# The sample's pointwise product: sixteen plain jobs of one token half each, or four units of seven block products

## The chip, the core and the metric

The kernel runs on one core of a Trainium2 chip. The metric is the device time of one execution in microseconds; three runs of the kernel before gave 2074.37, 2077.41 and 2079.27 us, and their median, 2077.41 us, is the time before.

## What is computed

One encoder layer is applied to two sequences that share all weights: a "sample" of 1024 tokens and a "prompt" of 512. All in fp32.

```python
def conformer_conv(u_val, u_glu, w_dw, b_dw, ln_g, ln_b, w_pw):
    h = u_val * jax.nn.sigmoid(u_glu)
    h = depthwise_conv(h, w_dw, 31 taps) + b_dw          # 1024 channels
    h = jax.nn.silu(layer_norm(h, ln_g, ln_b))
    return h @ w_pw                                       # 1024 x 1024

def mixer_layer(x, ...):
    z = rms_norm(x, norm_g) @ w_in                        # 2048 -> 5632
    c_val, c_glu, c_gate, q, k, v, a_gate = split(z)
    conv_out = conformer_conv(c_val, c_glu, ...) * silu(c_gate)
    attn_out = banded_sink_attention(rope(q), rope(k), v, sink) * silu(a_gate)
    return x + concat([conv_out, attn_out]) @ w_out       # 2048 -> 2048

y = rms_norm(mixer_layer(x), final_norm_g)                # for sample and prompt
```

The change is about `h @ w_pw`, the pointwise product, of the sample alone.

## The kernel before

**Layout and precision.** Channels lie on the 128 partitions, tokens along the free dimension. Every fp32 operand of a product is split into a high and a low part (`Encoder.parts`, L506: ScalarE copies the rounded high part at L510, VectorE subtracts it at L511), and a product of two blocks is three matmuls: high by high, high by low, low by high. Weights come as raw tiles of 512 KB (`raw`, 3 buffers) and become split tiles (`hl`, 3 buffers); split tokens are `t` tiles of 128 x 2 x 512 (`T1`, L456, 28 buffers). Other buffers: `f` (7 of 4 KB a partition), `a` (4), `g` and `u` (4 each of 2 KB a partition); `E()` (L477) hands out `g` and `u` in turn.

**Two ways to multiply.** A `Job` (L386) is one output block of 128 columns for 512 tokens: `Encoder.run` (L641) issues 3 matmuls for each input block, at L670. A `Unit` (L94) makes two column blocks for both halves of the sample's tokens from 8 input blocks, seen as a 2 x 2 by 2 x 2 block product, with seven products instead of eight (Winograd's form). Its token sums are S1 = A21 + A22, S2 = S1 - A11, S3 = A11 - A21, S4 = A12 - S2 (A12: first token half, second half of the input blocks). Its weight sums are made by VectorE from the two raw tiles (`sub`, L142-L163). Each of the seven products, in the order P1, P2, P6, P5, P7, P3, P4, is 4 input blocks x 3 matmuls of 512 columns, at L207. Three PSUM banks accumulate them, and after each product a `tap` (L230) takes the bank out: ScalarE copies (L236) and VectorE adds (L257); P7's bank is read before P4 accumulates into it one product later. `Onto` (L271) is the unit of the output projection: its four results start from tiles that GpSimd's queue loads, and VectorE adds every bank into them (L304).

**Order of the work.** The sample's input projection comes first (units, to about 850 us), then the prompt's 44 jobs `pj`, then the sample's pointwise product, then the sample's output projection (`over[0]`, `over[1]`: 16 `Onto` units), then the prompt's pointwise product and its output projection. Everything beside the products is written as generators in three lanes (`Lane`, L64). After every three matmuls `tick` (L517) gives each lane 648 ns times its rate of credit, and a lane steps while it has credit; each `yield` costs what it names. The lane `prep` runs at rate 1, `conv` (the prompt's depthwise taps, L1004) at 0.5 here, `attn` first sums up the sample's attention output (`attention_sums`, L1291: four rounds that each fill all four `a` tiles), then runs the prompt's attention (L1152). What weights and taps need is emitted with high priority; lane instructions stand behind it on VectorE and ScalarE. Every plain load and store goes over SP's queue in a fixed order; each engine's queue is in order too.

**The pointwise product of the sample.** From `pj[18]` (`prepare`, L2052) the `prep` lane runs `Post.prepare` (L1448) for each token half: layer norm and silu of the convolution's output, ending in a store to `cs_d` (L1500). Then `fetch` (L1505) loads the first half's 8 blocks back and splits them. For each half come 8 jobs (`first_jobs`, L1547): job i loads weights `w_pw[i]` (L404), the gate (`load_gate`, L1539), and multiplies the bank by the gate on VectorE (`pointwise`, L1530-L1533), then stores into `mix_d`. While the first half's jobs run, the second half is fetched; while the second half's run, `Mix.fill` (L1333) splits four of the seven token lots (4 tiles each) that the output projection's first unit needs; `rest` and the hooks after it (L2082-L2089) make the other three.

Of the kernel before, what the change touches and what calls it, by code (L numbers as in the profile page):

```python
# [7 lines left out]
F32 = mybir.dt.float32  # L8
F32R = mybir.dt.float32r
AF = mybir.ActivationFunctionType  # L10
ALU = mybir.AluOpType
PSUM = bass.MemoryType.PSUM

P = 128
# [26 lines left out]
LEAD = 9000  # L41
SPREAD = 3
RATES = (0.4, 0.6, 0.3, 1.0, 0.5)
S1, S2, S3, S4, S5, S6, S7, S8 = 5000, 6000, 9000, 7000, 3500, 2500, 6000, 6000
# [226 lines left out]
class Onto(Unit):  # L271
# [29 lines left out]
    def tap(self, name):  # L301
        n = self.START.get(name) or self.REST[name]
        d = self.d[n]
        self.e.nc.vector.tensor_tensor(d, self.bank[BANK[name]], d, ALU.add)  # L304
        if name in self.REST or name == "P4":
            del self.d[n]
            if self.total:
                self.done(n[0], n[1], d)
            else:
                self.e.store(self.part[n[0]][n[1]], d)  # L310


# [951 lines left out]
class Mix:  # L1264
# [67 lines left out]

    def fill(self):  # L1333

        e = self.e
        e.T = {}
        held = deque()

        def load(step):
            if step < 7:  # L1340
                held.append(self.load_sum(SUMS[ALONE[step]], 1, True, e.F))

        def put(step):
            for j, x in enumerate(held.popleft()):
                self.token_sum(SUMS[ALONE[step]], 1, j, x)

        load(0)
        load(1)
        for step in range(4):
            yield 2 * LOAD  # L1350
            put(step)
            load(step + 2)
        self.put, self.load = put, load

    def units(self):
        e = self.e
        out = []
        for o in range(0, ND, 2):
# [13 lines left out]
            out.append(one)  # L1372
        return out

    def project(self, o, t, z):
# [60 lines left out]


class Post:

# [3 lines left out]
    def __init__(self, e, seq, t0, out):  # L1443
        self.e, self.seq, self.t0, self.out = e, seq, t0, out
        self.cs, self.mix, self.made = {}, {}, {}
        self.cs_d = [e.tc.dram_tile([P, 2, self.N], F32, name=f"cs{seq.s}_{t0}_{i}") for i in range(NC // 2)]

# [51 lines left out]
    def normed(self, i, t):  # L1499
        self.e.store(self.cs_d[i], t)  # L1500
        self.kept = i + 1

    kept = 0

    def fetch(self):  # L1505

        e = self.e
        held = deque()

        def load(i):  # L1510
            if i < NC // 2:
                held.append(e.F([2, self.N]))
                e.nc.sync.dma_start(held[-1], self.cs_d[i])

        load(0)
        load(1)
        for i in range(NC // 2):
            yield LOAD
            t = held.popleft()
            load(i + 2)  # L1520
            for j in (0, 1):
                self.cs[2 * i + j] = self.parts(t[:, j])
                yield 1500

    def parts(self, f):
        t = self.e.T1([2, self.N])
        self.e.parts(t[:, 0], t[:, 1], f)
        return t

    def pointwise(self, i, acc):  # L1530
        e, nc = self.e, self.e.nc
        f = self.gates.pop(i)
        nc.vector.tensor_tensor(f, acc[0], f, ALU.mult)  # L1533
        self.mixed(i, f)

    def mixed(self, i, f):
        self.e.store(self.out.xT[i][:, self.t0 : self.t0 + self.N], f)

    def load_gate(self, i):  # L1539
        e = self.e  # L1540
        if i == 0:
            self.gates = {}
        f = e.G()
        e.nc.sync.dma_start(f, self.seq.gate_d[i][:, self.t0 : self.t0 + self.N])
        self.gates[i] = f

# [328 lines left out]
def encoder(ctx, tc, a):  # L1875
    e = Encoder(ctx, tc, a)
    sample, prompt = Sequence(e, 0), Sequence(e, 1)
    mix = Mix(e, sample, a["y_s"])
    halves = [Post(e, sample, 0, mix), Post(e, sample, TP, mix)]
    last = LastPost(e, prompt, 0, a["y_p"], mix.wsum_d)  # L1880
# [171 lines left out]
    def prepare():  # L2052
        until(lambda: sample.convolved == NC, e.conv)
        for half in halves:
            e.prep.add(half.prepare())
        e.prep.add(halves[0].fetch())
        e.attn.add(mix.attention_sums(prompt.fetch_first))
        for group in prompt.groups:
            e.attn.add(group)
# [6 lines left out]

    for n, half in enumerate(halves):
        fj = half.first_jobs()
        fj[0].before.insert(0, lambda half=half: until(lambda: len(half.cs) == NC, e.prep))
        if n == 0:  # L2070
            fj[0].before.append(lambda: e.prep.add(halves[1].fetch()))
        else:

            def fill():
                until(lambda: mix.gated == HALF, e.attn)
                e.prep.add(mix.fill())

            fj[0].before.append(fill)
        jobs += [[j] for j in fj]
    out = mix.units()  # L2080
    over = [[u(1, False) for u in out], [u(0, True) for u in out]]
    def rest():  # L2082
        e.prep.drain()
        mix.put(4)

    over[0][0].before.append(rest)
    over[0][0].after[0] = [lambda: (mix.put(5), mix.load(6))]
    over[0][0].after[1] = [lambda: e.prep.add(mix.conv_sums())]
    over[0][0].after[3] = [lambda: mix.put(6)]  # L2089
    over[0][-1].before += [e.prep.drain, e.attn.drain]  # L2090
# [17 lines left out]
    over[1][0].next = None  # L2108
    fj[-1].before.append(lambda: chain[0].begin((0, 0)))

# [67 lines left out]
```

## Time and profile before

| | |
|---|---|
| median of three runs | 2077.41 us |
| the profiled execution: its own time / its span | 2079.13 us / 2077.4 us |
| TensorE matmuls | 9256 recorded, busy 2060.1 us |
| VectorE / ScalarE / GpSimd busy | 1728.4 / 1081.8 / 157.9 us |
| DMA | 494.56 MB, mean 238 GB/s |
| sample's pointwise product on TensorE | from 1436.00 to 1536.06 us of the span |

The profile gives times in us from the start of the span. A matmul's end is modelled, so a run of matmuls is read by its starts. A row of the timeline is: start, duration, engine, line, operation, output <- inputs, how many were merged, and in brackets how long the engine sat idle before it and what ended that. A row of the stretches is: stretch, its length, busy time and count of each engine, granted clock, busy share of the 16 DMA engines, GB/s. A row of the groups is: line, engine, operation, shapes, count | busy us, mean ns of one | idle us before them and what ended it.

### The profile page before, as it was taken

To read this page: it belongs to the slowest core of one execution; us is meant where nothing else is said; L and a number is where in the kernel's file an instruction comes from. 1 tells how busy PE (TensorE), PEld (TensorE's weight loads), DVE (VectorE), ACT (ScalarE), POOL (GpSimd) and SP (SyncE) were. 2 spreads that over 40 slices of the span, in tenths; PEclk is the share of its full clock that TensorE was granted. 3 is DMA by queue.
4 is the path that set the end of the run, shared out by engine and by line. 5 is a ranking of instruction groups with operands and counts; after the bars stand their busy time and mean duration, and the time that the engine had idled before them with its cause. 6 is when DMAs were issued, how large, how long until landed. Compare 5 with 4: busy or idle time off the path is not lost.

```text
span 2077.4 us, 27223 instructions
## 1 busy us (share of the span) xinstructions
PE 2060.1 (99%) x9256; PEld 1697.9 (82%) x9256; DVE 1728.4 (83%) x2843; ACT 1081.8 (52%) x1771; POOL 157.9 (8%) x240
## 2 busy tenths in 40 slices
PE   9999999999999999999999999999999999999998
PEld 8888888888888888788888888888888887888886
DVE  8768899998899899889766777776799978998877
ACT  7486445333465555655555777336553343454454
POOL 0111111111112111100000000000000111100000
PEclk9999999999999999999999999999999999999999
DMA  8888886864577777954555555997789898778897
GB/s 285 309 300 256 200 215 226 286 218 158 190 243 197 181 167 179 279 167 158 164 183 185 178 172 188 316 329 233 239 295 295 279 324 283 213 259 277 293 324 279
DMA packets 242300, 494.56 MB, mean 238 GB/s; under 512 B 23664, under 2 KB 84464, under 8 KB 242160
## 3 DMA queue, kind: packets, MB, share of 16 engines
q1 hardware_dynamic: 216352, 428.83, 62.1%
q0 software_dynamic: 24512, 61.88, 12.5%
q10 hardware_dynamic: 1296, 2.11, 0.3%
q8 instruction: 72, 1.18, 0.2%
q14 instruction: 68, 0.56, 0.1%
HBM read 331.77 MB, written 160.96 MB: 237 GB/s over the span
## 4 chain that ended last, share of the span: by engine, by line
PE 73%; issue 8%; DMA 8%; DVE 7%; ACT 2%; POOL 1%; SPq 0%; ACTq 0%; POOLq 0%; DVEq 0%
PE a L207 21%; PE a L670 13%; PE c L207 10%; PE b L670 6%; PE c L670 6%; PE b L207 5%; PE s L1169 2%; PE pv L1198 2%; PE a L1852 2%; PE s L207 2%; DVE hl L511 2%; PE pt L1203 1%; PE s L1852 1%; DVE t L511 1%; DMA p<-y_d 1%
## 5 line engine op out<-in xcount | busy, mean ns | idle before, releaser
L207 PE MATMUL a<-t,hl 128*128 128x512 f32 x2640 | 632.5, 390 | 1.8 <-ACT u L236 1.3
L207 PEld LDWEIGHTS a<-t,hl 128*128 128x128 f32 x2640 | 493.5, 188 | 108.4 <-ACT u L236 2.4
L511 DVE TENSOR_TENSOR hl<-raw,hl 128x1024 fp32r<-128x1024 f32 (+3 forms) x334 | 337.8, 1012 | 151.5 <-ACT hl L510 147.3
L510 ACT ACTIVATE hl<-raw 128x1024 fp32r<-128x1024 f32 (+3 forms) x334 | 296.8, 889 | 314.4 <-PE c L207 88.1
L670 PE MATMUL a<-t,hl 128*128 128x512 f32 x1344 | 326.3, 393 | 0.0
L207 PE MATMUL c<-t,hl 128*128 128x512 f32 x1320 | 319.1, 389 | 0.0
L670 PEld LDWEIGHTS a<-t,hl 128*128 128x128 f32 x1344 | 248.8, 188 | 50.4
L207 PEld LDWEIGHTS c<-t,hl 128*128 128x128 f32 x1320 | 247.4, 188 | 51.5 <-DVE u L304 0.2
L1041 DVE SCALAR_TENSOR_TENSOR f<-f,c_w_dw,f 128x512 f32<-128x512 f32 x248 | 172.9, 744 | 0.2
L670 PE MATMUL b<-t,hl 128*128 128x512 f32 x672 | 162.9, 392 | 1.5 <-DVE t L515 0.8
L670 PE MATMUL c<-t,hl 128*128 128x512 f32 x672 | 163.9, 393 | 0.0
L1004 DVE SCALAR_TENSOR_TENSOR f<-f,c_w_dw,f 128x512 f32<-128x512 f32 x232 | 163.4, 742 | 0.2
L207 PE MATMUL b<-t,hl 128*128 128x512 f32 x660 | 159.8, 389 | 0.0
L670 PEld LDWEIGHTS b<-t,hl 128*128 128x128 f32 x672 | 124.8, 188 | 27.5 <-DVE t L515 1.1
L670 PEld LDWEIGHTS c<-t,hl 128*128 128x128 f32 x672 | 124.6, 188 | 24.8
L207 PEld LDWEIGHTS b<-t,hl 128*128 128x128 f32 x660 | 123.7, 188 | 25.6
L1033 DVE SCALAR_TENSOR_TENSOR f<-f,w_both,f 128x512 f32<-128x512 f32 x120 | 89.8, 748 | 2.0
L236 ACT ACTIVATE u<-a 128x512 f32<-128x512 f32 x82 | 48.8, 595 | 77.3 <-PE a L207 70.6
L236 ACT ACTIVATE g<-a 128x512 f32<-128x512 f32 x78 | 46.5, 596 | 78.5 <-PE a L207 68.5
L1183 ACT ACTIVATE p<-p,tiny 128x384 f32<-128x384 f32 (+1 forms) x96 | 54.6, 570 | 45.9 <-DVE tiny L1180 36.2
L510 ACT ACTIVATE a<-pt 128x512 fp32r<-128x512 f32 x64 | 38.0, 593 | 64.6 <-PE pt L1203 64.4
L285 POOL DMA_DIRECT2D g<-xT_s x16 | 8.8, 551 | 743.1 <-DMA att_d<-u 669.0
(356 smaller groups left out, 2765.2 us busy)
## 6 DMA issues: line engine op xcount, KB each, us to landing
raw<-w_in SPq DMA_DIRECT2D x170, 512.0 KB, 5.2
raw<-w_out SPq DMA_DIRECT2D x31, 512.0 KB, 5.1
raw<-w_pw SPq DMA_DIRECT2D x24, 512.0 KB, 4.2
wsum_P<-raw SPq DMA_DIRECT2D x47, 256.0 KB, 3.6
raw<-wsum_P SPq DMA_DIRECT2D x18, 512.0 KB, 5.1
f<-x_s SPq DMA_DIRECT2D x16, 512.0 KB, 8.5
g<-wsum_P SPq DMA_DIRECT2D x28, 256.0 KB, 4.6
a<-sum_S SPq DMA_DIRECT2D x24, 256.0 KB, 6.1
```

Of the source, the lines that this page charges most:

```text
L207: nc.tensor.matmul(acc, hl[:, l, o, j, :], toks[j][:, r], start=name in FRESH and j == 0 and q == 0, stop=name in LAST and j == HALF - 1 a ...
L236: nc.scalar.activation(t, bank, AF.Copy)
L510: nc.scalar.activation(hi, x, AF.Copy)
L511: nc.vector.tensor_tensor(lo, x, hi.bitcast(F32), ALU.subtract)
L670: nc.tensor.matmul(job.acc[0], hl[:, l, kk // HALF, kk % HALF, :], r, start=i == 0 and p == 0, stop=i == nk - 1 and p == 2,)
L1004: nc.vector.scalar_tensor_tensor(t, h[:, j : j + T], w(j), t, ALU.mult, ALU.add)
L1033: nc.vector.scalar_tensor_tensor(m0, odd[:, j : j + H], both(j), m0, ALU.mult, ALU.add)
L1041: nc.vector.scalar_tensor_tensor(out, d[:, j : j + H], w(2 * j + k), out if j else m0, ALU.mult, ALU.add)
L1169: nc.tensor.matmul(ps[:, 0:n], qs[:, x, h], k[y][:, keys], start=p == 0, stop=p == 2)
L1183: nc.scalar.activation(p[:, 0:n], p[:, 0:n], AF.Exp, bias=nm[:, h : h + 1], accum_out=l[:, h : h + 1])
L1198: nc.tensor.matmul(pv, v[x][:, vs], pt[:, y], start=i == 0 and p == 0, stop=i == last and p == 2)
L1852: nc.tensor.matmul(acc[t], self.toks[name, m][:, x, i, t * P : (t + 1) * P], parts[i][l].rearrange("p a b -> p (a b)"), start=fresh and fi ...
```

## The change

The sample's pointwise product is made by four units, one for each two columns of `w_pw`, over both token halves at once. A new class `Gated` (a `Unit`) loads the gates itself, two products ahead, over SP's queue, multiplies each finished result by its gate and stores it. A new class `Pointwise` holds the normed convolution's output in DRAM (`cs_d`), makes the sums S1 to S4 of block pairs by the generator that `Mix` has for its own (`conv_sums`, L1313: two loads of 512 KB, four VectorE operations, four stores of 256 KB for each of four pairs) and splits the first three token lots (`AHEAD`) while the prompt's jobs run; the last four lots are split before the first unit and after its first three products. The generators `fetch` and `fill` are gone; the output projection's token lots are split lot by lot behind the products of the last pointwise unit and the first output unit (`turn`). `conv_sums` of the output projection starts one product later.

```diff
+AHEAD = 3
+class Gated(Unit):
+    late = True
+    LASTS = {"P2": (0, 0), "P7": (1, 1), "P3": (0, 1), "P4": (1, 0)}
...
+    def begin(self, n):
+        self.g[n] = self.e.E()
+        self.e.nc.sync.dma_start(self.g[n], self.gate(*n))
+    def product(self, step, late):
+        if step == 0:
+            self.begin((0, 0))
+        name = self.order[min(step + 2, len(self.order) - 1)]
+        n = self.LASTS.get(name)
+        if n and n not in self.g:
+            self.begin(n)
+        return super().product(step, late)
+    def tap(self, name):
+        if name == "P4":
+            e, n = self.e, self.LASTS[name]
+            g = self.g[n]
+            e.nc.vector.tensor_tensor(g, self.bank[BANK[name]], g, ALU.mult)
+            e.store(self.to(*n), g)
+            self.g = {}
+        else:
+            super().tap(name)
+    def finish(self, n):
+        e, d = self.e, self.d.pop(n)
+        e.nc.vector.tensor_tensor(d, d, self.g[n], ALU.mult)
+        e.store(self.to(*n), d)
...
-    def fill(self):
...
+    def turn(self, unit, nxt, g):
+        held = {}
+        def load(step):
+            if step < 7:
+                held[step] = self.load_sum(SUMS[ALONE[step]], g, True, self.e.F)
+        def follow(step):
+            for j, x in enumerate(held.pop(step)):
+                self.token_sum(SUMS[ALONE[step]], g, j, x)
+            load(step + 2)
+        unit.before.append(lambda: (load(0), load(1)))
+        for step in range(7):
+            u, at = (unit, step + 2) if step < 5 else (nxt, step - 5)
+            u.after.setdefault(at, []).append(lambda step=step: follow(step))
...
+class Pointwise:
...
+    scale_of, sums_in_place, block_pairs = Mix.scale_of, Mix.sums_in_place, Mix.conv_sums
...
+    def ahead(self):
+        yield from self.block_pairs()
+        self.e.T = {}
+        self.load(0)
+        self.load(1)
+        for step in range(AHEAD):
+            yield 2 * LOAD
+            self.put(step)
+            if step + 2 < AHEAD:
+                self.load(step + 2)
+        self.ready = True
+    def units(self):
...
+        out = [one(i) for i in range(0, NC, 2)]
+        out[0].before.append(lambda: (self.put(AHEAD), self.load(AHEAD + 2)))
+        for step in range(AHEAD + 1, 7):
+            out[0].after[step - AHEAD - 1] = [lambda step=step: (self.put(step), self.load(step + 2))]
+        return out
...
     def normed(self, i, t):
-        self.e.store(self.cs_d[i], t)
+        for j in (0, 1):
+            self.e.store(self.out.xT[2 * i + j][:, self.t0 : self.t0 + self.N], t[:, j])
-    def fetch(self):
...
-        e.prep.add(halves[0].fetch())
+        e.prep.add(point.ahead())
...
+    def first_tokens():
+        until(lambda: point.ready, e.prep)
+        point.load(AHEAD)
+        point.load(AHEAD + 1)
+    pj[-2].before.append(first_tokens)
+    pw = point.units()
+    pw[-1].before.append(lambda: until(lambda: mix.gated == HALF, e.attn))
+    jobs += [[u] for u in pw]
...
+    mix.turn(pw[-1], over[0][0], 1)
+    over[0][0].after[2] = [lambda: e.prep.add(mix.conv_sums())]
...
+    pw[-1].after.setdefault(5, []).append(lambda: chain[0].begin((0, 0)))
```

## The prediction on record

> **What bounds the kernel.** I read the page first, its busy shares and its clock, then the stretches around the place of the change, then single matmuls in the timeline.
>
> ```profile
> span 2077.4 us, 27223 instructions
> PE 2060.1 (99%) x9256; PEld 1697.9 (82%) x9256; DVE 1728.4 (83%) x2843; ACT 1081.8 (52%) x1771; POOL 157.9 (8%) x240
> PEclk9999999999999999999999999999999999999999
> ```
>
> TensorE is busy in all but 17 us of the span, at full clock. VectorE, with 83%, is next. A busy TensorE may still be a slow one, so the second look is at its pace inside the stage that the change rewrites.
>
> ```profile
> 1525.18 5.60 PE L670 MATMUL c<-t,hl 128*128 128x512 f32 x24
> 1530.62 5.60 PE L670 MATMUL a<-t,hl 128*128 128x512 f32 x24
> 1536.06 2.88 PE L207 MATMUL a<-t,hl 128*128 128x512 f32 x12
> 1538.78 1.52 PE L207 MATMUL b<-t,hl 128*128 128x512 f32 x6
> ```
>
> The last two pointwise jobs start 5.44 us apart: 5.44/24 = 0.2267 us a matmul. The first product of a unit, 12 matmuls, takes 2.72 us to the next start: the same 0.2267. So neither form waits, and only fewer matmuls, or fewer waits elsewhere, can shorten the kernel. The stretches show what runs beside them.
>
> ```profile
> 1300.00:1350.00 50.00, 50.00 (x223) 41.39 (x222) 36.56 (x52) 15.96 (x19) 0.00 (x0) 1.00 0.91 314
> 1350.00:1400.00 50.00, 48.73 (x220) 40.08 (x219) 34.47 (x54) 16.28 (x22) 0.00 (x0) 1.00 0.94 333
> 1400.00:1436.00 36.00, 36.00 (x166) 30.10 (x165) 23.87 (x46) 25.14 (x44) 0.00 (x0) 1.00 0.70 228
> 1436.00:1536.00 100.00, 100.00 (x465) 83.31 (x464) 82.15 (x135) 53.34 (x93) 1.70 (x3) 1.00 0.79 264
> 1536.00:1600.00 64.00, 63.59 (x288) 51.04 (x287) 59.92 (x111) 27.46 (x54) 6.05 (x11) 1.00 0.87 283
> 1600.00:1650.00 50.00, 49.47 (x233) 41.44 (x234) 49.69 (x88) 17.90 (x33) 5.48 (x10) 1.00 0.90 288
> 1685.00:1735.00 50.00, 49.58 (x214) 39.59 (x213) 45.10 (x70) 27.42 (x43) 6.41 (x12) 1.00 1.01 339
> ```
>
> Three different limits lie side by side. From 1300 to 1400, the end of the prompt's jobs, the DMA engines are at 0.91 and 0.94 while VectorE has a quarter of its time free. In the pointwise stage (1436 to 1536) VectorE works 82 of 100 us. After it, in the output projection, VectorE is full (59.92 of 64.00, 49.69 of 50.00) and TensorE loses only 0.41 and 0.53 us.
>
> **What goes: matmuls.** Before: 2 halves x 8 jobs x 8 blocks x 3 = 384. After: 4 units x 7 products x 4 blocks x 3 = 336. 48 x 0.2267 = 10.9 us leave TensorE, which is never idle there (100.00 of 100.00). The attention's products between them (465 - 384 = 81 records) stay. This is the whole gain; the rest is what could eat it.
>
> **VectorE and ScalarE.** Prices, from the stage's groups, and one run of equal subtractions:
>
> ```profile
> L511 DVE TENSOR_TENSOR hl<-raw,hl 128x1024 fp32r<-128x1024 f32 x16 | 19.6, 1224 | 5.9 <-ACT hl L510 5.8
> L1004 DVE SCALAR_TENSOR_TENSOR f<-f,c_w_dw,f 128x512 f32<-128x512 f32 x40 | 28.2, 746 | 0.0
> ```
>
> ```profile
> 1700.47 2.48 DVE L511 TENSOR_TENSOR t<-a,t 128x512 fp32r<-128x512 f32 x4
> ```
>
> ```profile
> L510 ACT ACTIVATE t<-f 128x512 fp32r<-128x512 f32 x30 | 17.4, 621 | 5.7 <-DMA f<-msum_S 5.7
> L510 ACT ACTIVATE hl<-raw 128x1024 fp32r<-128x1024 f32 x16 | 16.9, 1058 | 23.2 <-PE a L670 14.1 <-PE b L670 4.8 <-PE c L670 3.6
> ```
>
> Four 512-column operations in 2.48 us, each 0.68 long, follow each other every 0.60 us; that is the price of one in a row. A 1024-column split costs 1.22. Before, VectorE spends 16 weight splits x 1.22 = 19.6, 16 token splits x 0.60 = 9.6 and 16 gate products x 0.60 = 9.6: 38.8 us. After, each unit needs two full splits (2.4), four weight sums and three half splits (4.2), three additions and four gate products (4.2): 10.8, four units 43.4; the pair sums 16 x 0.60 = 9.6; 28 token splits 16.8. Together 69.8, so 31 us more on an engine that has 349 free.
>
> By place: before the stage come 9.6 of pair sums and 12 splits, less the 8 splits of the first half, +12.0 us in 136 us of which 94.9 are used. There is room. In the stage itself 34.0 go (weight splits, 8 token splits, gates) and 43.4 + 16 x 0.60 = 53.0 come; the output's lots become five of seven instead of four, +2.4. The stage shrinks to 89.1 us, and what is paced by TensorE's progress (the other 38.6 us: prompt taps, attention) shrinks with it by 4.2. 82.15 - 34.0 + 53.0 + 2.4 - 4.2 = 99.4 us of work in 89.1. So about 10 us of VectorE's work must slide into a stage where it is full. What slides first is what stands behind the weights: the prompt's taps.
>
> ```profile
> L1004 DVE SCALAR_TENSOR_TENSOR f<-f,c_w_dw,f x232: 711/743/755, 1062.8 to 1658.9; 128x512 f32<-128x512 f32 x116
> ```
>
> They now end at 1658.9 and are asked for only before the third unit of `over[1]`, some 100 us later. But attention's splits slide too, and TensorE's fixed order waits for those. Bounds: 0 (all slack) to 10 us (all on the path). I take 2.0, about twice the 0.41 + 0.53 = 0.94 us that TensorE loses in the full stretches, for they are the nearest rows.
>
> ScalarE: 16 x 1.06 + 16 x 0.62 = 26.9 us before; 8 x 1.06 + 12 x 0.62 + 16 copies of a bank at 0.62 + 28 x 0.62 = 43.2 after. 16 more on 53.34 of 100 us: hidden, at nothing; if VectorE holds it up, that is in the 2.0.
>
> **The weights, gates and buffers.** Sixteen loads of 512 KB become eight; the gates stay 16 loads of 256 KB and the results 16 stores, on SP as before, so the loads that stand behind them meet no longer queue. A unit holds up to six `g` and `u` tiles, a weight sum and a query: eight of eight. Should the copy of P7's bank miss a tile, P4 waits. Over the whole span TensorE's waits for such copies are:
>
> ```profile
> PE a L207 <- ACT u L236: 1.3, 2, 1.1
> PE a L207 <- ACT g L236: 0.3, 1, 0.3
> ```
>
> So the bounds are 0 and, with the longest of them once in each of four units, 4.4 us. I take 0, for the span shows three such waits in all, with the same unit order and as few buffers.
>
> **The prompt's last jobs.** When does the new work run? The lane charges one half's `prepare` 72,000 ns, both 144,000, the pair sums 4 x 13,000, the three lots 3 x 9,000: 223,000. A prompt job pays 16 x 648 = 10,368. That is 21.5 jobs after `pj[18]`, so in `pj[39]`; the forced stepping before `pj[42]` finds nothing left, and costs nothing. In time:
>
> ```profile
> L504 SPq DMA_DIRECT2D cs<-t x8: 319/324/660, 1188.3 to 1309.0; - x8
> L1513 SPq DMA_DIRECT2D f<-cs x8: 319/432/453, 1275.0 to 1440.4; - x8
> ```
>
> The pair sums start once the second half is stored, after 1309, and take 52,000/10,368 = 5 jobs, 55 us; the lots follow to about 1395. This lies squarely on the stretch where the DMA engines are full. Added there: 8 loads of 512 KB, 16 stores and 12 loads of 256 KB, 11.5 MB, less one fetch of 0.5: 11.0 MB. What fits: 339 GB/s at a share of 1.01, 333 at 0.94 and 314 at 0.91 mean 336 to 354 at full, say 345; beside the 323 of these 100 us that leaves 2.2 MB. The other 8.8 MB take 25 us and must be pushed into 1400 to 1436 (228 GB/s) and later. Who waits for them?
>
> ```profile
> L1305 DVE TENSOR_TENSOR a<-a,a 128x1024 f32<-128x1024 f32 x8 | 9.8, 1224 | 20.4 <-DMA a<-ag_d 20.4
> ```
>
> ```profile
> 1389.51 1.23 DVE L1305 TENSOR_TENSOR a<-a,a 128x1024 f32<-128x1024 f32 x1 [0.75 <-DMA a<-ag_d]
> ```
>
> ```profile
> 1390.77 0.63 ACT L510 ACTIVATE a<-p 128x512 fp32r<-128x512 f32 x1 [4.84 <-DVE a L1305]
> ```
>
> ```profile
> 1391.45 0.50 PE L1169 MATMUL s<-f,a 128*128 128x256 f32 x2 [0.51 <-ACT a L510]
> 1392.71 0.73 PE L1169 MATMUL s<-f,a 128*128 128x256 f32 x4 [0.76 <-DVE a L511]
> ```
>
> VectorE already stands 20.4 us waiting for the gates of the sample's attention, with weight splits behind it in its queue. The last round's product frees the `a` tile that the prompt's first query is split into (ScalarE stood 4.84 us for it), and TensorE waits 0.51 and 0.76 us for that split. So this chain has no slack: a later landing there is a wait of TensorE. Bounds: 0, if the new transfers give way (the first tokens are needed only at 1430), to 25. I take 2.5, twice the 1.27 us of today, as the weights have two half jobs of lead and the lots are not urgent; this is the softest number here.
>
> On the room itself the Trainium skill (HBM Reference, Specifications) speaks the other way: a core that streams alone reaches about 425 GB/s, and 358 only when both of a pair stream. One core runs here; by that page (425 - 323) x 100 us, some 10 MB, would fit, and this term would be nearly 0. The 339 GB/s at a share of 1.01 does not bear that out for transfers of this kernel's sizes, so I keep the term and give the case where all fits a smaller chance.
>
> **Sum.** 10.9 - 2.0 - 2.5 = 6.4 us. From the profiled execution's own time, 2079.13 (span 2077.4 and 1.7 around it), that makes 2072.7. This execution lies 1.7 above the median of the three runs, 2077.41; against the median I forecast **2071.0 us**.
>
> **Rivals.** *All is hidden*: the transfers find room or give way, and late taps hurt nobody. 2077.4 - 10.9 = 2066.5. For it: TensorE loses under 1 us beside a full VectorE and full DMA engines today. Against: the two waits at 1391.
>
> *VectorE becomes the bound*: the 10 us of excess reach TensorE through attention's splits and through the token lots of the last pointwise unit. There four splits (2.4 us) join 10.8/7 = 1.5 of the unit and some 1.4 of lanes in each product, 5.3 us of work in 2.72. Similar crowding at 1685 to 1735 cost 0.42 us, but without taps and attention. Then 2077.4 - 10.9 + 10 + 2.5 = 2079.0: no change.
>
> *Slower*: the DMA crowding from 1309 on delays the last round of attention sums, and TensorE waits for the first product of L1169. Half to all of the 25 us is 12.5 to 25; I price it at 17, and 2.0 for VectorE stays: 2077.4 - 10.9 + 19.0 = 2085.5. It decides above 13.1 us of wait (10.9 - 2.0 + 4.2). For it: no slack there, and queues in fixed order. Against: all buffers of both lanes are few, so they throttle themselves. Such a break can cost clock as well:
>
> ```profile
> 1904.72 5.60 PE L670 MATMUL a<-t,hl 128*128 128x512 f32 x24
> 1910.85 1.84 PE L701 MATMUL s<-ones,f 128*128 128x1 f32 x16
> 1912.55 7.65 PE L1852 MATMUL a<-hl,t 128*128 128x512 f32 x24
> ```
>
> After 1.84 us of one-column products 24 matmuls took 7.65 us instead of 5.60: 2 us more for each such break, within the 17. The Trainium skill (TensorE: Matmul & The Clock Gate, Part 1) says that the clock halves only after an idle window of about 3.4 us; by it the 2 us fall away for shorter waits. Here a shorter pause did it.
>
> **Chances.** Forecast 0.44, all hidden 0.17, VectorE the bound 0.21, slower 0.18. What a measurement of this kernel can tell from no change is about 0.2%, 4.2 us: the runs before lie 4.9 apart. The first two are faster by more (0.61), the third is the same (0.21), the last slower (0.18). The range takes in the full gain with 1.5 us for scatter, 2065.0, and the lower half of the slower case (12.5 us of wait, 2081.0) with 2 us of scatter, 2083.0; the forecast's own range, with 1 to 7 us eaten, is 2067.5 to 2073.5.
>
> **What would show it.** Right: 336 matmuls of L207 in place of 384 of L670, units 19.04 us of matmul starts apart (7 x 2.72) plus attention; VectorE above 95% in the stage; the waits of TensorE for L1169 and L1198 summing to 3 to 7 us; the last tap (L1004) later than 1659 less the gain. Wrong: TensorE idle over 10 us before 1436 (the slower rival), long waits for `t` at the switch to the output projection (VectorE), or waits for a bank's copy (the buffers).

## The result and the profile after

The changed kernel takes 2111.29 us (median of four runs, 2108.61 to 2112.08) against 2076.32 for the kernel before: a ratio of 1.0165, 95% interval 1.0147 to 1.0183. It is 35 us slower; 6 us faster was forecast, and the range ended at 2083.0. The profiled execution took 2108.61 us. The page's first lines:

```profile
span 2106.8 us, 27244 instructions
PE 2062.5 (98%) x9208; PEld 1689.6 (80%) x9208; DVE 1761.6 (84%) x2903; ACT 1095.5 (52%) x1802; POOL 157.5 (7%) x240
```

48 matmuls are gone, as foreseen, and yet TensorE's idle time grew from 17 to 44 us. VectorE has 33 us more (31 were worked out). The stretches tell where; their bounds follow the new stages: the prompt's last jobs end at 1445.5, the four units last to 1555.5, the first two units of the output projection to 1609.8.

```profile
1300.00:1350.00 50.00, 50.00 (x222) 41.41 (x221) 31.76 (x44) 14.93 (x16) 0.00 (x0) 1.00 0.91 319
1350.00:1400.00 50.00, 42.01 (x177) 33.71 (x176) 26.01 (x36) 11.10 (x12) 0.00 (x0) 0.93 0.96 350
1400.00:1445.50 45.50, 42.83 (x192) 34.53 (x191) 41.38 (x69) 21.22 (x29) 0.00 (x0) 1.00 0.93 323
1445.50:1555.50 110.00, 100.34 (x443) 77.72 (x442) 97.66 (x177) 72.81 (x144) 0.00 (x0) 0.98 0.67 217
1555.50:1609.80 54.30, 46.91 (x191) 35.72 (x190) 48.91 (x85) 23.22 (x43) 5.53 (x10) 0.94 0.84 276
1609.80:1750.00 140.20, 139.38 (x637) 115.15 (x637) 131.23 (x227) 60.76 (x109) 15.89 (x29) 1.00 0.91 303
```

Three stretches lose, and the last one shown loses no more than before. Measured by stage, TensorE reaches the first unit 9.5 us late (1445.5 for 1436.0); the units take 110.0 us where the sixteen jobs took 100.1; the two output units take 54.3 us, 46.2 before. Beyond its matmuls at their usual spacing (0.2267 us for 512 columns) the stretch from 1300 to the first unit loses 14.0 us, the units 17.1 and the two output units 13.5; before, it was 2.2, 0.6 and 2.4. This is what "loses" means below. In the first place VectorE is *less* busy than before from 1350 to 1400 (26.01 us against 34.47): it did not have too much to do, it stood still. VectorE's timeline shows at what, and the rows of ScalarE and TensorE beneath belong to it:

```profile
1379.99 1.22 DVE L1345 TENSOR_TENSOR a<-a,a 128x1024 f32<-128x1024 f32 x1 [1.23 <-DMA a<-ag_d]
1386.74 1.23 DVE L1345 TENSOR_TENSOR a<-a,a 128x1024 f32<-128x1024 f32 x1 [5.53 <-DMA a<-ag_d]
...
1391.88 0.69 DVE L1366 TENSOR_TENSOR f<-f,f 128x512 f32<-128x512 f32 x1 [0.62 <-DMA f<-cs_d]
...
1394.66 1.22 DVE L551 TENSOR_TENSOR hl<-raw,hl 128x1024 fp32r<-128x1024 f32 x1
```

```profile
1383.85 1.06 ACT L550 ACTIVATE hl<-raw 128x1024 fp32r<-128x1024 f32 x1 [3.92 <-PE a L710]
```

```profile
1395.93 12.06 PE L710 MATMUL b<-t,hl 128*128 128x512 f32 x46 [6.23 <-DVE hl L551]
```

ScalarE had its half of the next weights by 1384.9. VectorE's half came 9.8 us later, because its queue had stopped at a product of the attention sums (L1345) whose gate had not landed, and the rest of that round and a pair sum (L1366) stood ahead too. TensorE waited 6.23 us, and then needed 12.06 us for 46 matmuls (10.4 at 0.2267). In the units and at the switch there are many small waits; the longest rows of TensorE's waits there, first for the units, then for the switch:

```profile
PE a L208 <- ACT u L237: 3.1, 1, 3.1
PE a L208 <- ACT hl L550: 1.4, 2, 1.2
PE a L208 <- DVE hl L551: 1.1, 1, 1.1
PE c L208 <- DVE t L551: 0.9, 2, 0.5
```

```profile
PE a L208 <- ACT t L550: 2.1, 1, 2.1
PE a L208 <- DVE u L305: 1.9, 2, 1.6
PE b L208 <- DVE t L551: 1.3, 1, 1.3
```

### The profile page after: what moved, and what is told of

Same layout as the page of the kernel before. It is cut to its first block, busy times and chain, and to the rows that moved or that the text cites. A ratio compares the mean times of both kernels' runs of the same rounds, so it can differ in the third digit from the quotient of the medians.

```text
span 2106.8 us, 27244 instructions
## 1 busy us (share of the span) xinstructions
PE 2062.5 (98%) x9208; PEld 1689.6 (80%) x9208; DVE 1761.6 (84%) x2903; ACT 1095.5 (52%) x1802; POOL 157.5 (7%) x240
## 4 chain that ended last, share of the span: by engine, by line
PE 74%; DMA 8%; issue 7%; DVE 6%; ACT 3%; POOL 1%; SPq 1%; ACTq 0%; POOLq 0%; DVEq 0%
PE a L208 23%; PE c L208 11%; PE a L710 10%; PE b L208 6%; PE c L710 5%; PE b L710 5%; PE pv L1238 2%; PE a L1899 2%; PE s L1209 2%; PE s L208 2%; PE s L1899 2%; PE pt L1243 1%; DVE hl L551 1%; PE pt L208 1%; DMA a<-ag_d 1%
## 5 line engine op out<-in xcount | busy, mean ns | idle before, releaser
L208 PE MATMUL a<-t,hl 128*128 128x512 f32 x2832 | 687.3, 392 | 13.5 <-ACT u L237 3.4
L208 PEld LDWEIGHTS a<-t,hl 128*128 128x128 f32 x2832 | 530.6, 189 | 131.7 <-ACT u L237 5.1
L551 DVE TENSOR_TENSOR hl<-raw,hl 128x1024 fp32r<-128x1024 f32 (+3 forms) x334 | 333.5, 999 | 145.4 <-ACT hl L550 144.2
L208 PE MATMUL c<-t,hl 128*128 128x512 f32 x1416 | 346.6, 392 | 1.2 <-DVE t L551 0.9
L208 PEld LDWEIGHTS c<-t,hl 128*128 128x128 f32 x1416 | 266.0, 188 | 58.8 <-DVE t L551 2.5
L710 PEld LDWEIGHTS a<-t,hl 128*128 128x128 f32 x1152 | 212.7, 188 | 47.3 <-ACT g L1088 2.1
L208 PE MATMUL b<-t,hl 128*128 128x512 f32 x708 | 174.0, 390 | 1.3 <-DVE t L551 1.3
L208 PEld LDWEIGHTS b<-t,hl 128*128 128x128 f32 x708 | 132.6, 188 | 28.7 <-DVE t L551 1.7
L710 PE MATMUL b<-t,hl 128*128 128x512 f32 x576 | 141.1, 395 | 7.9 <-DVE hl L551 6.7
L710 PEld LDWEIGHTS b<-t,hl 128*128 128x128 f32 x576 | 108.1, 190 | 31.3 <-DVE hl L551 7.5
L237 ACT ACTIVATE g<-a 128x512 f32<-128x512 f32 x86 | 51.2, 596 | 85.7 <-PE a L208 75.7
```

What stands on the lines that cost most here:

```text
L208: nc.tensor.matmul(acc, hl[:, l, o, j, :], toks[j][:, r], start=name in FRESH and j == 0 and q == 0, stop=name in LAST and j == HALF - 1 a ...
L237: nc.scalar.activation(t, bank, AF.Copy)
L551: nc.vector.tensor_tensor(lo, x, hi.bitcast(F32), ALU.subtract)
L710: nc.tensor.matmul(job.acc[0], hl[:, l, kk // HALF, kk % HALF, :], r, start=i == 0 and p == 0, stop=i == nk - 1 and p == 2,)
```

## The experiments

My first theory: three places, each an in-order queue of its own. At the prompt's end the DMA traffic of the pair sums holds VectorE's queue; in the units ScalarE's softmax stands in front of bank copies that have one product of time; at the switch the token lots are too much for VectorE at once. The rivals are VectorE's load everywhere, and missing `g` and `u` tiles. All kernels are the changed one with one edit, unless said otherwise. The stages are read from the starts of L208's matmuls in one execution of each kernel, which can lie off the median (by 7.7 us with the query loaded late). The difference in the last column is that of the two ratios times 2077 us; a ratio is good to 3 to 6 us, so a difference to about 5 to 7, and a smaller one is not shown. The kernels that leave out pair sums (whole or half), lots' loads, start tiles or taps compute another result.

| kernel | median us | ratio to before, 95% | first unit at | four units | next two units | against the changed kernel |
|---|---|---|---|---|---|---|
| before | 2076.3 | 1 | 1436.0 | 100.1 | 46.2 | -34 |
| changed | 2111.29 | 1.0165 (1.0147 to 1.0183) | 1445.5 | 110.0 | 54.3 | 0 |
| no pair sums | 2093.06 | 1.0071 (1.0056 to 1.0086) | 1443.5 | 95.6 | 53.8 | -20 |
| attention stopped | 2130.85 | 1.0254 (1.0239 to 1.0270) | 1449.6 | 91.5 | 61.3 | +18 |
| copies on VectorE | 2117.21 | 1.0191 (1.0176 to 1.0206) | 1444.5 | 105.0 | 66.9 | +5 |
| query loaded late | 2109.72 | 1.0159 (1.0142 to 1.0176) | 1443.1 | 108.7 | 52.4 | -1 |
| lots a product earlier | 2106.72 | 1.0140 (1.0123 to 1.0157) | 1447.6 | 109.2 | 50.5 | -5 |
| taps put off | 2117.99 | 1.0194 (1.0179 to 1.0209) | 1445.2 | 104.4 | 53.4 | +6 |
| faster preparation | 2112.75 | 1.0166 (1.0151 to 1.0181) | 1463.6 | 95.5 | 54.8 | 0 |
| the last three together | 2120.22 | 1.0207 (1.0190 to 1.0225) | 1463.6 | 91.5 | 56.0 | +9 |
| longer lead | 2129.53 | 1.0247 (1.0224 to 1.0271) | 1436.4 | 103.0 | 60.3 | +17 |
| four loads of seven | 2108.83 | 1.0148 (1.0127 to 1.0168) | 1444.3 | 107.2 | 53.4 | -4 |
| lots over GpSimd's queue | 2113.39 | 1.0169 (1.0151 to 1.0187) | 1446.9 | 109.2 | 54.2 | +1 |
| softmax behind copies | 2120.27 | 1.0205 (1.0188 to 1.0222) | 1443.5 | 110.0 | 52.1 | +8 |
| pair sums without bytes | 2095.69 | 1.0087 (1.0072 to 1.0102) | 1439.8 | 100.7 | 54.1 | -16 |
| bytes without pair sums | 2111.44 | 1.0162 (1.0147 to 1.0177) | 1447.7 | 108.9 | 55.3 | -1 |
| lighter switch | 2102.64 | 1.0122 (1.0107 to 1.0137) | 1445.2 | 108.3 | 49.2 | -9 |
| lighter switch, no pair sums | 2086.04 | 1.0039 (1.0025 to 1.0054) | 1442.2 | 94.7 | 49.3 | -26 |
| taps left out | 2104.70 | 1.0121 (1.0094 to 1.0148) | 1446.5 | 106.2 | 47.3 | -9 |
| the last two together | 2077.95 | 1.0004 (0.9993 to 1.0016) | 1444.6 | 89.5 | 42.9 | -33 |

### The pair sums: their work or their bytes

```diff
-        yield from self.block_pairs()
...
-            if name in ("S1", "S2", "S3", "S4"):
+            if name in ("S1", "S2", "S3", "S4") and (g, name) in self.sums_d:
```

> The changed kernel without the sums of block pairs (no loads, sums or stores of them; the token lots S1 to S4 of the pointwise product are read as plain blocks instead, so its result is another). This takes 4.2 MB of loads, 4.2 MB of stores and 9.6 us of VectorE's subtractions out of the end of the prompt's jobs. Theory, crowded DMA engines hold up VectorE's queue there: the first unit starts at about 1436 us in place of 1445.5, the waits of TensorE for split weights before it fall from 11 us to under 2, and the two later clusters stay: about 2100 us. Rival, too much work for VectorE over the whole stage: the first unit starts at 1443 or later, what is won comes after it, 2106 or more.

20 us come back, but not where the theory put them: the units lose 7.0 us in place of 17.1, and the first one starts only 2 us earlier (the stretch before it loses 9.2 us in place of 14.0). The pair sums matter, and their place in the theory falls. Two more kernels keep one half of them each. One loads a single pair and sums it four times, storing nothing; the other loads and stores all, and sums nothing:

```diff
+        for t, k in zip(x, (0, HALF)):
+            nc.sync.dma_start(t, self.xT[k])
+        for j in range(HALF):
+            yield 2 * LOAD
+            nc.vector.tensor_tensor(d, b, d, ALU.add)
...
```

> The changed kernel with the 16 subtractions and additions of the pair sums on VectorE, but with one pair loaded in place of four and no sum stored (7.3 of 8.4 MB left out; the token lots read plain blocks, so the result is another). Without pair sums at all the kernel took 2093. Theory, their bytes and loads delay others at the prompt's end: as without them, 2092 to 2098. Rival, their 9.6 us on VectorE: near the changed kernel, 2105 or more.

```diff
-    scale_of, sums_in_place, block_pairs = Mix.scale_of, Mix.sums_in_place, Mix.conv_sums
+    def sums_in_place(self, g, j, x0, x1):
+        a, b, c, d = x0[:, :W], x0[:, W:], x1[:, :W], x1[:, W:]
+        for name, t in (("S1", d), ("S3", b), ("S2", a), ("S4", c)):
+            self.e.store(self.sums_d[g, name][j], t)
```

> The other half: all loads and stores of the pair sums, but no subtraction on VectorE (the unsummed blocks are stored, so the result is another). VectorE never waits for these loads then. If it is VectorE's queue standing for them (8.6 us of waits in the changed kernel), the time falls to 2095 to 2100; if it is the bytes, by which the attention sums' loads and the first tokens come late, it stays at 2106 to 2113.

Without the bytes 16 us come back, without the work 1. The stretch from 1350 to 1400, first without the bytes, then without the work, and for the latter what VectorE did:

```profile
1350.00:1400.00 50.00, 50.00 (x222) 41.39 (x221) 34.61 (x47) 14.96 (x17) 0.00 (x0) 1.00 0.94 331
```

```profile
1350.00:1400.00 50.00, 44.79 (x189) 36.22 (x188) 13.88 (x19) 10.01 (x11) 0.00 (x0) 0.97 0.93 342
```

```profile
1381.66 1.23 DVE L1345 TENSOR_TENSOR a<-a,a 128x1024 f32<-128x1024 f32 x1 [7.90 <-DMA a<-ag_d]
1388.02 1.23 DVE L1345 TENSOR_TENSOR a<-a,a 128x1024 f32<-128x1024 f32 x1 [5.14 <-DMA a<-ag_d]
```

VectorE works 34.61 us in the first and TensorE never waits; it works 13.88 us in the second, and TensorE loses 5 us, with 5 more behind 1400. So it is the transfers and not the sums on VectorE. In the run with the bytes alone VectorE cannot stand for the pair sums' own loads; it stands for those of the attention sums. It stands for them no longer in all than it did before (16.1 us in the changed kernel, 18.3 with the bytes alone, 20.4 in the kernel before, from 1300 to the first unit), but at another time, with the split of the next weights due. For the third round of attention sums is issued some 20 us later. Its first and last load on SP's queue, in the kernel before and in the changed one:

```profile
1348.80 0.84 SPq L1300 DMA_DIRECT2D a<-att_d  x1
1354.18 0.53 SPq L1301 DMA_DIRECT2D a<-ag_d  x1
```

```profile
1369.13 0.44 SPq L1340 DMA_DIRECT2D a<-att_d  x1
1378.41 0.43 SPq L1341 DMA_DIRECT2D a<-ag_d  x1
```

Without the bytes the first of them goes out at 1353.05. From issue to landing a gate's load takes hardly longer (median 8.1 us, 7.3 before). So most of the delay arises before the issue, in SP's one fixed order or in `a` tiles that come back late, and less in slow transfers. These two were not separated: no run put the pair sums on another queue.

Could the traffic be moved in time? Twice the time between the loads of a round of attention sums and their use:

```diff
-            yield e.attn.rate * 1.5 * LEAD
+            yield e.attn.rate * 3 * LEAD
```

> The changed kernel with 27 us in place of 13.5 us between the loads of a round of attention sums and their first product. Theory, VectorE's queue is held at the prompt's end by products whose loads have not landed, with the split of the next weights behind them: VectorE's waits for those loads fall from 16 us to under 5, the loss before the first unit from 14 to under 6; attention starts some 40 us later and weighs on the output projection: 2098 to 2106. Rival, the bytes themselves are too many for the stretch: weights and tokens land late instead, the loss before the first unit stays over 10, 2108 or more.

```profile
1350.00:1400.00 50.00, 50.00 (x222) 41.43 (x221) 33.44 (x48) 15.11 (x17) 0.00 (x0) 1.00 0.93 332
1400.00:1440.00 40.00, 33.22 (x140) 27.04 (x140) 24.32 (x36) 13.68 (x19) 0.00 (x0) 0.91 0.90 317
```

The loss before 1400 is gone, but at 1423.76 TensorE waits 6.78 us for a bank's copy (L1088) on ScalarE, which had stood 6.90 us for a load of the first token lots (`f<-csum_S`, until 1419.54). The first unit starts on time, the units lose 17.2 us as before and the two output units 16.0, and the time grows by 17. VectorE's waits for the gates did not fall (18.4 us). Both expectations missed the total. Earlier pair sums instead:

```diff
+    pace(pj[PM], 1.3, e.prep)
...
+    pace(pw[0], 1.0, e.prep)
```

> The changed kernel with the preparation lane at rate 1.3 in place of 1.0 from the prompt's 18th job to the first pointwise unit, so that the pair sums and the first token lots are made some 40 us earlier, where the DMA engines are at 0.53 to 0.60. Theory, crowded DMA engines at the prompt's end hold up VectorE's queue: the 14 us lost between 1300 and the first unit fall under 6, and the first unit finds its tokens; 2095 to 2103. Rival, the attention sums alone stall VectorE there: 10 us or more still lost, 2106 to 2112.

No change in the total, close to what the rival named: VectorE now stands 25.6 us for the gates of the attention sums, 12.1 us at once. The prompt's end loses 23 us instead of 14, the units 7 instead of 17.

### The units: softmax, buffers, VectorE

The longest single wait there has this queue before it on ScalarE:

```profile
1463.10 1.28 ACT L1223 ACT_TABLE_LOAD   x1
1464.39 0.61 ACT L1223 ACTIVATE p<-p,tiny 128x384 f32<-128x384 f32 x1
...
1466.80 0.19 ACT L1224 ACTIVATE tiny<-tiny 128x4 f32<-128x4 f32 x1
1466.90 0.57 ACT L237 ACTIVATE u<-a 128x512 f32<-128x512 f32 x1
```

Four kernels bear on it: attention stopped, the copies on VectorE, the query's `u` tile held for a shorter time, and softmax at ordinary priority.

```diff
+    pace(pw[0], 0.0, e.attn)
...
+    over[0][0].after[4] = [lambda: setattr(e.attn, "rate", 2.0)]
```

> The changed kernel with the attention lane stopped from the first pointwise unit to the fifth product of the output projection's first unit, then at rate 2.0. Theory, softmax on ScalarE and attention's splits stand in front of bank copies that have one product (2.7 us) of time: from the first unit's start to the last unit's end TensorE loses under 4 us in place of 17, at the switch to the output projection under 7 in place of 13; attention then crowds the output projection, which may lose 5 to 15 us, so the whole is open between 2093 and 2110. Rival, the units themselves are too dense (their own weights, sums, gates, few buffers): over 10 us lost in the units all the same.

```diff
+            if isinstance(self, Gated):
+                nc.vector.tensor_copy(t, bank)
```

> The changed kernel with the 16 bank copies of the pointwise units on VectorE in place of ScalarE. Theory, ScalarE's queue: the waits for the copies go, 4 to 8 us back, 2103 to 2107 us. Rival, VectorE is the bound of the stage: 16 x 0.6 = 9.6 us more on it show in full, 2116 to 2121. Rival, missing g and u tiles: no change, as the same tiles are held as long, 2109 to 2113.

```diff
-        self.load_query(g, b + 1)
...
+            if i == 0:
+                self.load_query(g, b + 1)
             yield S5
```

> The changed kernel with the query of the next attention block loaded some 10 us before it is used, not at the start of the block before, so that it holds a u tile for a third of the time. Rival, the units' copies and gates miss u tiles: 4 to 8 us back, 2103 to 2107. Theory, ScalarE's queue: within 2 us of the changed kernel, 2109 to 2113.

```diff
-        with e.tc.high_priority(SOON):
+        with e.tc.high_priority(SOON) if self.s == 0 else ExitStack():
             nc.vector.tensor_scalar(nm, m, -1.0, None, ALU.mult)
```

> The changed kernel with the prompt's softmax at ordinary priority, so that in ScalarE's queue the bank copies of the units stand before the exponentials and not behind them. Theory, a bank copy behind 3.8 us of softmax stops TensorE: the longest wait in the units (3.1 us, for a copy) and the slow matmuls after it go, 3 to 6 us back, 2105 to 2108. Rival, the copy waits for its u tile: no change, 2109 to 2113.

Without further attention the units still lose 10.6 us, so the theory of ScalarE's queue falls as the main cause; the total, 2131 us, lies outside the range given, and the two output units take 61.3 us. With the copies on VectorE the total (2117) is the one that the VectorE rival named, yet the units take 5 us less and the next two 13 more, so the 9.6 us do not show where they were added. The late query gains 1 us, which is not clear of noise. With softmax behind the copies the 3.1 us wait is gone, another, of another kind, is longest from the first unit to the end of the switch, and the kernel is 8 us slower, which neither expectation had:

```profile
PE c L208 <- DVE t L551: 11.8, 2, 8.6
PE a L208 <- ACT u L237: 1.9, 1, 1.9
```

The wait for the copy was real, but behind it stood the next one. Missing `u` tiles are not shown as a cause, but a gain of up to 6 us by them is not excluded. What the units win without the pair sums (10 of 17 us) shows that most of their loss came with the pair sums; that it reached them by tokens, splits and jobs that arrive late is argued, not measured.

### The switch to the output projection

```diff
-            u, at = (unit, step + 2) if step < 5 else (nxt, step - 5)
+            u, at = (unit, step + 1) if step < 6 else (nxt, step - 6)
```

> The changed kernel with the output projection's seven token lots split one product (2.7 us) earlier each. Theory, VectorE: 28 token splits (16.8 us) and a unit's own 10.8 us, beside taps and attention, meet in 19 us of matmuls, so moving them by one product gives back about one product at most: 1 to 3 us, 2108 to 2110. Rival, the lots are merely asked for too late: the 13 us lost in the two units from the switch on fall under 7, 2103 to 2105.

```diff
+    pace(pw[0], 0.0)
...
+    over[0][0].after[3] = [lambda: setattr(e.conv, "rate", 0.8)]
```

> The changed kernel with the prompt's depthwise taps stopped from the first pointwise unit to the fourth product of the output projection's first unit, and at rate 0.8 in place of 0.5 from there. Theory, VectorE is the bound at the switch and near it in the units: taps are about 0.66 us of VectorE for every 1.5 us there; without them the loss at the switch falls from 13 to under 6 us and in the units from 17 to under 11; some 3 us come back to be paid in the output projection: 2095 to 2102. Rival, loads and queues: less than 4 us in all, 2107 or more.

> The three edits together: lots one product earlier, no taps beside the units, faster preparation. If the three places are independent, the gains add: 2108 to 2110, 2095 to 2102 and 2095 to 2103 against 2111 give 2076 to 2094. If VectorE's total is what binds, what one place gives the next one takes, and it comes out above 2098.

The earlier lots win 5 us, between the two expectations and at the edge of the noise, 3 to 4 of them at the switch. Taps put off win 5.6 us in the units and 0.9 at the switch, and cost more later, so that the total is 6 us worse: at the next change of tokens TensorE waits once for 11.4 us.

```profile
PE a L208 <- DVE t L551: 11.4, 1, 11.4
```

Together the three do not add, as the rival had it: the switch, freed of taps, has one wait of 11 us in place of several. In each of them ScalarE stands for the lots' loads (`f<-msum_S`). So the loads:

```diff
-            if step < 7:
+            if step < 7 and step % 2 == 0:
...
-            for j, x in enumerate(held.pop(step)):
+            for j, x in enumerate(held[step - step % 2]):
```

> The changed kernel with four loads in place of seven for the output projection's first token lots: lots 2, 4 and 6 are split again from the tiles of lots 1, 3 and 5 (so its result is another); every split on ScalarE and VectorE stays. Theory, with only two lots in flight the loads set the pace of the switch (about 5 us a lot against 2.7 us a product): the loss in the two units from the switch on falls from 13 to under 6, 2101 to 2105. Rival, VectorE sets it (27.6 us of splits and a unit's own work in 19 us): over 10 still lost, 2109 or more.

```diff
-            e.nc.sync.dma_start(x, src)
+            (queue or e.nc.sync).dma_start(x, src)
```

> The changed kernel with the seven lots of the switch loaded over GpSimd's queue in place of SP's. If what delays them is SP's queue (the keys, values and queries of attention and the stores in front of them), the loss at the switch falls from 13 to under 8 and the time to 2103 to 2107. If the four tiles that they are loaded into set the pace, nothing changes, 2109 to 2113.

Neither does it alone: 4 us won and 1 lost are both within the noise, and the two output units still lose 12.5 and 13.3 us. With four loads the next late thing is the start tile of the first result, for which `begin`, on GpSimd's queue, waits until a pointwise unit's tile has been stored.

```profile
1551.77 0.58 POOL L286 DMA_DIRECT2D g<-xT_s  x1 [693.09 <-DMA mix_d<-g]
```

```profile
1559.56 0.69 DVE L305 TENSOR_TENSOR u<-a,u 128x512 f32<-128x512 f32 x1 [2.30 <-DMA u<-xT_s]
```

So both at once: four loads, and a first output unit that starts from its products alone.

```diff
+            if not self.bare:
+                self.e.nc.gpsimd.dma_start(self.d[n], self.source(*n))
...
+        if self.bare and name in self.START:
+            self.e.nc.vector.tensor_copy(d, self.bank[BANK[name]])
```

> The changed kernel with two things lighter at the switch to the output projection: four loads for the seven token lots (as in the run with fewer loads), and the output's first unit starts from its products alone, without loading its four start tiles (so the input is not added in two columns, and three lots are others). Theory, two loads are late there by about as much, so that taking one away uncovers the other: together the loss in the two units from the switch on falls from 13 to under 6 us, 2102 to 2105 us. Rival, VectorE's amount of work: still over 10 us, 2108 or more.

> The lighter switch and no pair sums, together. If the two places are independent: 2093 less 7 to 9 us, 2083 to 2087, so that some 10 us of the loss at the prompt's end and in the units stay unexplained. If a stall freed at one place moves to the next, 2090 or more.

9 us come back where the fewer loads alone gave 4, and the two output units lose 8.4 us in place of 13.5, not under 6. Both places add: 20 + 9 against 26 measured. What is left at the switch of the combined run is a full VectorE (third number pair of its row):

```profile
1536.90:1586.20 49.30, 44.44 (x192) 33.24 (x191) 47.76 (x84) 19.99 (x38) 3.35 (x6) 1.00 0.74 235
```

Hence the last pair, with the taps beside the units not put off but left out:

```diff
+            if not e.skip:
                 nc.vector.scalar_tensor_tensor(t, h[:, j : j + T], w(j), t, ALU.mult, ALU.add)
```

> The changed kernel with the prompt's taps left out (not put off) from the first pointwise unit to the end of the output projection's second unit, some 48 operations and 34 us of VectorE, so that the prompt's result is another. Put off instead of left out they gave 7 us back here and cost 13 later. Theory, loads are late first and VectorE's load comes second: 4 to 9 us back, 2102 to 2107. Rival, VectorE's load alone makes the units' and the switch's loss: 20 us or more back, below 2092.

> The run with the lighter switch and no pair sums (2086), and the same taps left out. There VectorE is busy in 47.8 of the 49.3 us of the switch. Theory, what is left there is VectorE's load: the loss at the switch falls from 8 to under 4 us and in the units from 6 to under 4, 2076 to 2081. Rival, something else holds the units: 2084 or more. All without waits would be 2077 - 11 = 2066.

The theory's numbers are met in both: 9 us back alone, 7 on top of the others. The stretches of the last run are the units, the switch and what follows:

```profile
1444.60:1534.10 89.50, 89.50 (x418) 74.08 (x417) 73.14 (x130) 62.85 (x118) 0.00 (x0) 1.00 0.68 224
1534.10:1577.00 42.90, 42.23 (x195) 34.70 (x194) 39.74 (x74) 18.47 (x35) 3.35 (x6) 1.00 0.91 291
1577.00:1750.00 173.00, 168.05 (x751) 137.53 (x750) 144.10 (x242) 71.55 (x127) 19.21 (x35) 0.99 0.87 286
```

The units now run without a wait in 89.5 us; the prediction had the stage at 89.1. No kernel that computes the whole reference beat the one before; the best was that with earlier lots, 2106.72.

## Why the prediction was wrong

**The gain** was right: 336 matmuls, and, once nothing else stands in the way, a stage of 89.5 us for 100.1. 

**The step that failed is the term for the prompt's last jobs**, "I take 2.5", from bounds of 0 to 25. It measured 16 (their bytes) to 20 us (all of the pair sums), 5 to 9 of them at the prompt's end itself and 8 to 10 in the units. The traffic behind it was written down: 11.0 MB where, by its estimate, 2.2 fit. The reason for the small value, that "the weights have two half jobs of lead and the lots are not urgent", is what fell: the splits of the weights stand in VectorE's queue behind the sums whose loads are late (1386.74 to 1394.66), so a transfer that nobody needs soon delays what TensorE needs now. I took twice the wait that I saw, 1.27 us, when the DMA engines were already at 0.94. The surplus that did not fit, 25 us, was nearer to the result, but that it sets the 16 to 20 us is not shown, as the loads were mainly issued late.

**VectorE's 2.0 us** (bounds 0 and 10) was probably too small as well: 7 to 9 us come back with the taps left out. That edit takes 34 us off VectorE, over three times the excess of 10 us that had been worked out, so it tells what VectorE's load costs in these stages, and only bounds what the excess alone does. VectorE reached 97.66 of 110.00 us in the units, 89%, not the 95% named as a sign; it stood there mainly for ScalarE (3.5, 3.0 and 2.9 us in the three longest groups) and 1.4 us for a load. The last tap came late, as foreseen:

```profile
L1044 DVE SCALAR_TENSOR_TENSOR f<-f,c_w_dw,f x232: 716/744/752, 1064.9 to 1712.6; 128x512 f32<-128x512 f32 x116
```

**The switch's loads were not in the sum at all.** I counted five lots' splits there for VectorE, but not that 28 token tiles are needed by the units to their end, so that the lots can no longer be split ahead, and that their loads and the start tiles now hang on buffers just given back: 9 us in the whole time, 5 of them in the two output units.

**Buffers and ScalarE at nothing:** the longest wait for a bank copy was 3.1 us, inside the 4.4 that I gave as bound, but it was ScalarE's queue and not a tile; no edit won it back by itself.

**The rivals.** The slower one had the right cause, later attention sums, in another place: not TensorE at L1209's first product (L1169 before) but at the weights. Its 17 us meet the 16 to 20 in part by luck, for they were meant for the prompt's end alone, where 11.8 us more are lost than before. The wait that it named is there once the pair sums are gone; in the last run (L1216 there is L1209) it is the longest before the units:

```profile
PE s L1216 <- ACT a L556: 3.3, 1, 3.3
```

Its sign came: from 1300 to the first unit TensorE is idle for 10.7 us (145.5 less 50.00, 42.01 and 42.83). Its 2085.5 fell short because it kept VectorE at 2.0 and knew of no late loads at the switch. Summed from the runs: -10.9 + 18 + 9 + 8 = 24 of the 34 us, each term good to about 5; the other 10 to 12, what the last run lacks to 2066.5, stay at the prompt's end (first unit at 1444.6 even then) and after 1577, where 4.95 us of idle time stand in the row above. Which transfer holds those was not settled.

**The crowding itself.** The prediction set the Trainium skill's 425 GB/s (HBM Reference, Specifications) against 345 GB/s from the rows. In the changed kernel 350 GB/s go with a share of 0.96, 365 at full by that ratio. But within that stretch, from 1353.25 to 1364.00, it moves 399 GB/s at a share of 1.02, and the kernel before moves 411 from 110 to 130, so a full share has no one rate here, and 345 was too low a ceiling. The room was not used: from 1290 to 1400 the changed kernel moves 36.4 MB, the one before 35.5. The case "all hidden", which rested on room, falls with the 16 us that the bytes cost.

## What to carry to other kernels

Where the DMA engines are already at 0.9, do not price new transfers by the waits that stand there before, and look for their cost on the path, whoever they belong to: in-order queues hand the delay to the most urgent instruction behind. When a change fills the buffers that let the next stage be prepared, cost that stage's loads anew. And expect small waits to stand in line: one edit of one cause won little at the switch, two together won what they hid.

## What the runs showed of the hardware

Short waits cost clock. At the switch, after waits of 1.59, 0.60 and 2.07 us, matmuls follow each other every 0.4 us:

```profile
1564.56 1.19 PE L208 MATMUL a<-t,hl 128*128 128x512 f32 x4 [1.59 <-DVE u L305]
1566.35 3.51 PE L208 MATMUL a<-t,hl 128*128 128x512 f32 x8 [0.60 <-DVE t L551]
1571.93 0.50 PE L208 MATMUL a<-t,hl 128*128 128x512 f32 x1 [2.07 <-ACT t L550]
1572.27 4.28 PE L208 MATMUL c<-t,hl 128*128 128x512 f32 x11
```

8 in 3.51 us and 11 in 4.28, where 0.2267 each would make 1.8 and 2.5. The granted clock was 0.50 from 1566.01 to 1569.42 and again from 1572.84 to 1576.25, 3.41 us each time, and 1.00 between. In the 3.41 us before the first of these TensorE was busy for 1.56 us, before the second for 1.35. The prediction had such a case after 1.84 us; the Trainium skill (TensorE: Matmul & The Clock Gate, Part 1) speaks of an idle window of about 3.4 us, and no single wait here is as long.
